# Decoder layer: one 512-wide sum moved behind a split, two norms and the mixer's adds put in another order

## The chip, the cores and the metric

The kernel runs on one core of a Trainium2 chip. The metric is device microseconds of one execution. TensorE (PE) multiplies, VectorE (DVE) and ScalarE (ACT) prepare operands and finish results, GpSimd (POOL) and SyncE (SP) mostly start transfers.

## The reference

One decoder layer on 256 tokens of width 2048: a half-step SwiGLU feed-forward (FFN, 5632 wide), a mixer with two attention branches that are gated and projected, a second half-step FFN. After each of the three parts the residual sum goes through a layer norm.

```python
def _layer_norm(x, g, b):
    mu = jnp.mean(xf, axis=-1, keepdims=True)
    var = jnp.mean(jnp.square(xf - mu), axis=-1, keepdims=True)
    return (xf - mu) * lax.rsqrt(var + LN_EPS) * g + b
...
def _swiglu(x, w_gate, w_up, w_down):
    return (jax.nn.silu(x @ w_gate) * (x @ w_up)) @ w_down
...
    y = jax.nn.sigmoid(gate_mla) * (o_mla @ w_br_mla) + jax.nn.sigmoid(gate_diff) * (o_diff @ w_br_diff)
    return y @ w_out
```

All of it is float32.

## The kernel before, in words

**Products.** Each float32 product is made of three matmuls on rounded halves (`triple`, lines 205 to 207): high by high, high by low, low by high. A matmul takes a 128x128 block of activations and 128x512 of weights. Activations are kept as 128x128 blocks with the features on the partitions, for two blocks of 128 tokens, "block 0" and "block 1".

**Splits.** Every weight block, 128x1024 (two steps of the contraction), is loaded by SP into a `raw` tile and split into two `wring` tiles: ACT casts the high part (line 152), DVE subtracts it from the raw block for the low part (line 153). The pairs come from a ring of 6 or 10. `unit` puts a block's load, its split (`prep`) and its matmuls (`now`) into a pipeline; `later(n, f)` calls f after n more such steps, and `catch_up` does the matmuls of block 1 that lag behind those of block 0.

**Order.** A scheduler of the framework orders each engine's instructions from the program and from its own costs. `tc.issue_after(i)` adds a rule: what is in its scope comes behind instruction i on that engine. It is an order, not a wait on another engine. What is issued waits for its operands, and all that stands behind it on the same engine waits too.

**Gate/up groups.** After the first two column blocks, done by `project`, the gate and up weights are taken in groups p = 1 to 10 by `Hybrid.group`, which saves products by a seven-form scheme: some products are made of sums of weight blocks (line 405, tiles `sraw`, 128x1024, steps s = 0 and 1) and of sums of activations. Groups with p % 3 != 1 are "wide": they have a third step s = 2 with a 128x512 block (tiles `eraw`, the "e" sum, split and product). Forms 5, 6 and 4 have such sums; in the FFN this makes six wide groups each, p = 2, 3, 5, 6, 8, 9. Splits there stand in a fixed line (`split_in_line`), and `behind_split(n)` puts a sum behind the n-th last split of that line. The mixer's gates and its dq, dk and dv projections use the same group with `small`, without the e part.

**Norms.** `LayerNorm.evac` adds a finished bank of the last projection to the residual rows `z` (line 749 or 751) and counts statistics. After the last one `apply` computes the root on ACT (line 661), its inverse on DVE (lines 667 to 676, `f`), scales `z` (line 784), and `rows_to_quad` turns it for the next projections: PE transposes (line 647) and ACT applies gain and shift (line 652). The rows that the next residual needs are finished with gain and shift in two DVE operations each (lines 790 and 791). A dummy root (line 743) loads ACT's table ahead of time. The first norm stands between the first FFN and the mixer, the second behind the projection `w_out`, whose products of block 1 lag those of block 0; the second FFN's gate/up products on block 0 begin meanwhile.

Of the kernel before, what the change touches and what calls it, by code (L numbers as in the profile page):

```python
# [18 lines left out]
P = 128  # L19
# [40 lines left out]
def layer_kernel(ctx: ExitStack, tc: tile.TileContext, a: dict, out: bass.AP):  # L60
# [55 lines left out]
    class Acts:  # L116
        def __init__(self, k, name, kept=()):
            self.name = name
            self.kept = kept
            self.tiles = {}  # L120
            self.ready = set()
            self.made = {}
            self.raws = {}

# [12 lines left out]
        def put(self, q, b, src, i0=0, n=4):  # L137
            hi, lo = self.quad(q, b)
            hi, lo = hi[:, i0:i0 + n, :], lo[:, i0:i0 + n, :]
            if len(src.shape) == 4:  # L140
                hi, lo = (v.rearrange("p k (i c) -> p k i c", i=4) for v in (hi, lo))
            self.made[q, b] = split(hi, lo, src)
            self.ready.update((4 * q + i0 + i, b) for i in range(n))

# [3 lines left out]

    cast = [None]

    def split(hi, lo, src):
        cast[0] = S.copy(hi, src)  # L152
        return V.tensor_tensor(out=lo, in0=src, in1=hi.bitcast(F32), op=ALU.subtract)  # L153

# [185 lines left out]
    class Hybrid:  # L340
# [14 lines left out]

        def group(self, w0, w1, done, wide=False, seeded=False):
            banks = {}
# [35 lines left out]
            def seventh(p, s):  # L393
# [7 lines left out]
                def prep():  # L401
                    t = R[src][s]
                    if add is not None and (small or p != 7):
                        with nullcontext() if small else behind_split(s + 1):
                            V.tensor_tensor(out=t, in0=t, in1=R[add[1]][s], op=ALU.add)  # L405
# [20 lines left out]
            def plain(n, j, last=False):  # L426
# [13 lines left out]
                def now():  # L440
# [202 lines left out]

    def rows_to_quad(src, b, x, q, gain=None, shift=None):
        t = tr_bank()
        for i in range(4):
            PE.transpose(t[:, i * P:(i + 1) * P], src[:, i * P:(i + 1) * P], ident)
        if gain is not None:
            full = x.raw(q, b) if q in x.kept else tmp_tile([P, 512], "full")
            for i in range(4):  # L650
                k = 4 * q + i
                S.activation(full[:, i * P:(i + 1) * P], t[:, i * P:(i + 1) * P], AF.Identity,
                             bias=shift[:, k:k + 1], scale=gain[:, k:k + 1])
            t = full
        x.put(q, b, t.rearrange("p (i t) -> p i t", i=4))

    def rstd(v, eps, n, between=None):
# [3 lines left out]
        S.activation(sd, ve, AF.Sqrt, scale=4.0)  # L661
        w = sm(n, "w")
# [43 lines left out]
    class LayerNorm:  # L706
        def __init__(self, scale, residual, g, bt, each, x=None, cols=None, at=((0, 2, 4, 6), (8, 11, 14, 17)), root_at=1):
            self.scale = scale
            self.root_at = root_at
            self.x = x  # L710
# [8 lines left out]
            self.gb = [[None, None] for _ in range(2)]  # L719
            self.applied = {}  # L720

            def rows(h, b):
# [41 lines left out]
        def apply(self, b):  # L764
# [5 lines left out]
            if self.cols is None:  # L770
# [10 lines left out]
                return  # L781
            r = rstd(mv[:, 1:2], LN_EPS, 1)
            for c in range(4):
                self.applied[b] = V.tensor_scalar(out=zs[c], in0=zs[c], scalar1=mv[:, 0:1], scalar2=r,
                                                  op0=ALU.subtract, op1=ALU.mult)
                rows_to_quad(zs[c], b, self.x, c, *self.cols)
# [9 lines left out]
    def ffn(n, x, wgu, wdn, residual, g, bt, each, first=None, between=None, nxt=None, cols=None):  # L796
        hb = {}
# [59 lines left out]
        project(wgu[0], x, KD, 512, lambda b, bank: gu_done(0, b, bank), hook=first_hook,  # L857
                between=between, behind_x=3 if n == 2 else None)
        project(wgu[1], x, KD, 512, lambda b, bank: gu_done(1, b, bank), hook=second)
        look(3, 4)  # L860
        hy = Hybrid(x, seven, KD, extra=extra)
        for p in range(1, KF // 4):
            if p == KF // 4 - 1:
                for i, q in enumerate((3, 4, 0)):
# [5 lines left out]
                     p % 3 != 1, p > 1)  # L870
        ln = LayerNorm(0.5, residual, g, bt, each, nxt, cols, ((24, 26, 48, 50), (94, 97, 100, 103)), 35)
        if n == 1:
# [164 lines left out]
    def mixer(x):  # L1037
# [71 lines left out]
        for i, f in ((0, 0), (1, 0), (0, 2)):  # L1109
            w = (a["wgm"], a["wgd"])[i]  # L1110
            hy.group(w[f], w[f + 1], lambda n, b, bank, snap, op, i=i, f=f: keep_gate(i, f + n, b, bank, snap, op),
                     False, f == 2)

# [215 lines left out]
    h2 = Acts(KD, "h2", (0, 1, 2))  # L1329
    ln = LayerNorm(1.0, res[0], a["ln2_g"], a["ln2_b"], keep(1), h2, a["ln2_cols"])  # L1330
# [91 lines left out]
```

## Time and profile before

| | us |
|---|---|
| median of 3 runs | 1981.29 |
| lowest and highest | 1980.22, 1982.05 |
| profiled execution's own time | 1981.89 |
| its span, first to last instruction | 1979.8 |
| PE busy | 1960.8 |
| DVE busy | 1756.0 |
| ACT busy | 1261.4 |
| POOL busy | 294.3 |

The profile is of one execution. Its span leaves out 2.1 us of that execution's own time. A row of a timeline gives start, duration, engine, line, operation, and out<-in; `x2` means that two like instructions stand in one row; what stands in brackets is the idle time before it and what ended that. The granted clock of PE is 0.999 over the span.

### The profile page before, as it was taken

How to read it: one execution, taken by the hardware profiler on the slowest of the kernel's cores; microseconds unless marked ns; L12 is line 12 of the kernel's file. 1: busy time of each engine (PE TensorE's matmuls, PEld its weight loads, DVE VectorE, ACT ScalarE, POOL GpSimd, SP SyncE). 2: the span in 40 equal slices, each digit the busy share in tenths (PEclk: the TensorE clock that was granted, in tenths of full speed). 3: DMA queues.
4: the chain of work that ended last, by engine and by line, in shares of the span. 5: the costliest groups of instructions: out<-in, count | busy, mean ns of one | idle time of the engine just before them, and what ended most of it. 6: DMA issues, size and time to landing. Idle time of an engine off the chain costs nothing.

```text
span 1979.8 us, 25620 instructions
## 1 busy us (share of the span) xinstructions
PE 1960.8 (99%) x8796; PEld 1621.2 (82%) x8796; DVE 1756.0 (89%) x2135; ACT 1261.4 (64%) x1637; POOL 294.3 (15%) x515
## 2 busy tenths in 40 slices
PE   9999999999999999999999999999999999999997
PEld 7888888888888798888788888878888888888886
DVE  7999999999998889998877676699999999989886
ACT  6666666766655566666667765566676666666552
POOL 0221112112100011002223120012112121121000
PEclk9999999999999999999999999999999999999999
DMA  8978888778777666677667667579888877787763
GB/s 303 292 234 272 273 257 252 226 221 316 252 231 260 216 214 242 220 250 250 219 209 249 232 216 273 183 245 289 240 290 268 243 241 238 214 323 256 245 214 125
DMA packets 144594, 484.63 MB, mean 245 GB/s; under 512 B 20640, under 2 KB 20688, under 8 KB 144464
## 3 DMA queue, kind: packets, MB, share of 16 engines
q1 hardware_dynamic: 112752, 389.60, 57.2%
q0 software_dynamic: 31712, 93.41, 17.7%
q8 instruction: 69, 1.13, 0.2%
q14 instruction: 61, 0.50, 0.1%
HBM read 454.08 MB, written 28.84 MB: 244 GB/s over the span
## 4 chain that ended last, share of the span: by engine, by line
PE 48%; DVE 3%; issue 1%; DMA 1%; ACT 1%; POOL 0%; DVEq 0%; POOLq 0%; ACTq 0%
PE mm L206 15%; PE mm L207 15%; PE mm L205 15%; DVE wring L153 2%; DVE sraw L405 1%; DMA turn<-blocks 1%; PE tr L205 0%; PE tr L207 0%; PE tr L206 0%; POOL turn L684 0%; ACT wring L152 0%; DMA turned<-turn 0%; DVE blocks L682 0%; PE tr L1229 0%; PE tr L1231 0%
## 5 line engine op out<-in xcount | busy, mean ns | idle before, releaser
L152 ACT CAST wring<-raw 128x1024 fp32r<-128x1024 f32 (+2 forms) x475 | 490.6, 1038 | 340.7 <-PE mm L207 249.4
L153 DVE TENSOR_TENSOR wring<-raw,wring 128x1024 fp32r<-128x1024 f32 (+2 forms) x475 | 566.9, 1200 | 121.1 <-ACT wring L152 118.1
L152 ACT CAST wring<-sraw 128x1024 fp32r<-128x1024 f32 x436 | 452.0, 1051 | 191.9 <-DVE sraw L405 76.5
L153 DVE TENSOR_TENSOR wring<-sraw,wring 128x1024 fp32r<-128x1024 f32 x436 | 520.9, 1218 | 26.7 <-ACT wring L152 24.6
L207 PE MATMUL mm<-wring,h 128*128 128x512 f32 (+2 forms) x1260 | 484.7, 385 | 0.0
L206 PE MATMUL mm<-wring,h 128*128 128x512 f32 (+2 forms) x1260 | 484.3, 385 | 0.1
L205 PE MATMUL mm<-wring,h 128*128 128x512 f32 (+2 forms) x1260 | 483.8, 385 | 0.4 <-ACT h L152 0.4
L206 PE MATMUL mm<-wring,xs 128*128 128x512 f32 x776 | 303.1, 391 | 1.8 <-DVE wring L153 1.2
L205 PE MATMUL mm<-wring,xs 128*128 128x512 f32 x776 | 302.3, 390 | 0.0
L207 PE MATMUL mm<-wring,xs 128*128 128x512 f32 x776 | 302.0, 389 | 0.0
L206 PEld LDWEIGHTS mm<-wring,h 128*128 128x128 f32 x1260 | 236.7, 188 | 47.7 <-DVE wring L153 1.4
L205 PEld LDWEIGHTS mm<-wring,h 128*128 128x128 f32 x1260 | 236.7, 188 | 47.4 <-ACT h L152 0.9
L207 PEld LDWEIGHTS mm<-wring,h 128*128 128x128 f32 x1260 | 236.7, 188 | 47.2 <-DVE h L153 0.7
L405 DVE TENSOR_TENSOR sraw<-sraw,sraw 128x1024 f32<-128x1024 f32 x168 | 199.3, 1217 | 3.5 <-DMA sraw<-in_wdv_dram 2.4
L206 PEld LDWEIGHTS mm<-wring,xs 128*128 128x128 f32 x776 | 145.7, 188 | 35.7 <-DVE wring L153 5.6
L205 PEld LDWEIGHTS mm<-wring,xs 128*128 128x128 f32 x776 | 145.7, 188 | 30.3
L207 PEld LDWEIGHTS mm<-wring,xs 128*128 128x128 f32 x776 | 145.7, 188 | 29.8
L206 PE MATMUL mm<-wring,x 128*128 128x512 f32 x348 | 135.9, 390 | 0.7 <-DVE wring L153 0.7
L205 PE MATMUL mm<-wring,x 128*128 128x512 f32 x348 | 135.1, 390 | 0.7 <-ACT wring L152 0.5
L207 PE MATMUL mm<-wring,x 128*128 128x512 f32 x348 | 135.3, 389 | 0.0
L684 POOL DMA_DIRECT2D hT<-blocks x176 | 96.8, 562 | 186.4 <-DVE blocks L682 186.4
L407 POOL DMA_DIRECT2D sraw<-in_gu_dram x40 | 35.5, 887 | 511.7 <-DVE sraw L405 406.2
(301 smaller groups left out, 2210.4 us busy)
## 6 DMA issues: line engine op xcount, KB each, us to landing
raw<-in_gu_dram SPq DMA_DIRECT2D x167, 512.0 KB, 5.1
sraw<-in_gu_dram SPq DMA_DIRECT2D x160, 512.0 KB, 5.3
raw<-in_dn_dram SPq DMA_DIRECT2D x140, 512.0 KB, 4.8
sraw<-in_gu_dram POOLq DMA_DIRECT2D x40, 512.0 KB, 7.0
sraw<-in_dn_dram SPq DMA_DIRECT2D x36, 512.0 KB, 6.2
hraw<-hT POOLq DMA_DIRECT2D x68, 256.0 KB, 5.7
raw<-in_w_out_dram SPq DMA_DIRECT2D x32, 512.0 KB, 4.3
eraw<-in_gu_dram SPq DMA_DIRECT2D x48, 256.0 KB, 5.7
```

Of the source, the lines that this page charges most:

```text
L152: cast[0] = S.copy(hi, src)
L153: return V.tensor_tensor(out=lo, in0=src, in1=hi.bitcast(F32), op=ALU.subtract)
L205: PE.matmul(o, xh, wh, start=first, stop=False, skip_group_check=again)
L206: PE.matmul(o, xh, wl, start=False, stop=False, skip_group_check=again)
L207: PE.matmul(o, xl, wh, start=False, stop=last, skip_group_check=again)
L405: V.tensor_tensor(out=t, in0=t, in1=R[add[1]][s], op=ALU.add)
L407: nc.gpsimd.dma_start(R["12"][s], source("22", s), accum_op=ALU.add)
L684: nc.gpsimd.dma_start(to.rearrange("(g r) (i f) -> i r g f", g=4, i=4)[i], t[32 * i:32 * (i + 1), :].rearrange("r (g f) -> r g f", g=4))
```

## The change

Four edits. In the lists below a row is a place in an engine's order, with its line and its tiles.

**Gate/up.** An e sum (s = 2) is put behind the second last split of the line and no longer behind the third last. `behind_split(s + 1)` becomes `behind_split(min(s + 1, 2))`.

DVE in form 6 of the third group (p = 3), before; `sraw_460`, `sraw_461` and `eraw_468` are the weights of the three steps, `raw_1155` is the next plain block:

```order
139 L405 TENSOR_TENSOR sraw_460<-sraw_460,sraw_464 128x1024
140 L405 TENSOR_TENSOR sraw_461<-sraw_461,sraw_465 128x1024
141 L405 TENSOR_TENSOR eraw_468<-eraw_468,eraw_469 128x512
142 L153 TENSOR_TENSOR wring_115<-sraw_460,wring_114 128x1024
143 L153 TENSOR_TENSOR wring_105<-sraw_461,wring_104 128x1024
144 L153 TENSOR_TENSOR wring_103<-eraw_468,wring_102 128x512
145 L153 TENSOR_TENSOR wring_121<-raw_1155,wring_120 128x1024
```

And now, on the same engine:

```order
139 L416 TENSOR_TENSOR sraw_460<-sraw_460,sraw_464 128x1024
140 L416 TENSOR_TENSOR sraw_461<-sraw_461,sraw_465 128x1024
141 L155 TENSOR_TENSOR wring_115<-sraw_460,wring_114 128x1024
142 L155 TENSOR_TENSOR wring_105<-sraw_461,wring_104 128x1024
143 L416 TENSOR_TENSOR eraw_468<-eraw_468,eraw_469 128x512
144 L155 TENSOR_TENSOR wring_103<-eraw_468,wring_102 128x512
145 L155 TENSOR_TENSOR wring_121<-raw_1155,wring_120 128x1024
```

The e sum moved from ahead of two splits to right ahead of its own. ACT's casts at the same place, before:

```order
115 L152 CAST wring_104<-sraw_461 128x1024
116 L152 CAST wring_102<-eraw_468 128x512
117 L152 CAST wring_116<-sraw_463 128x1024
118 L152 CAST wring_114<-eraw_468 128x512
119 L152 CAST wring_104<-sraw_466 128x1024
```

And now (`wring_102` is the pair of form 6's e block, `wring_114` here that of form 7's):

```order
115 L154 CAST wring_104<-sraw_461 128x1024
116 L154 CAST wring_116<-sraw_463 128x1024
117 L154 CAST wring_114<-eraw_468 128x512
118 L154 CAST wring_102<-eraw_468 128x512
119 L154 CAST wring_104<-sraw_466 128x1024
```

The cast of form 6's e block moved behind two others. The same stands in groups 6 and 9 and in the second FFN.

**First norm.** Its finishing steps are no longer ordered behind the scaling of block 1, and the dummy root is called at the first FFN's column 2 of block 0, without a rule. In ACT's order it now stands before the tables of the sines and exponentials, and a table load stands directly ahead of the real root. DVE at block 0's root, before:

```order
709 L153 TENSOR_TENSOR wring_103<-raw_5483,wring_102 128x1024
710 L667 RECIPROCAL y_5257<-sd_5253 128x1
711 L670 SCALAR_TENSOR_TENSOR t_5259<-y_5257,w_5255 128x1
712 L153 TENSOR_TENSOR wring_121<-raw_5500,wring_120 128x1024
713 L676 SCALAR_TENSOR_TENSOR f_5261<-t_5259,y_5257 128x1
714 L153 TENSOR_TENSOR wring_119<-raw_5516,wring_118 128x1024
```

And now; the scaling is line 808:

```order
709 L687 RECIPROCAL y_5257<-sd_5253 128x1
710 L690 SCALAR_TENSOR_TENSOR t_5259<-y_5257,w_5255 128x1
711 L696 SCALAR_TENSOR_TENSOR f_5261<-t_5259,y_5257 128x1
712 L808 TENSOR_SCALAR z_3860<-z_3860,mv_5249,f_5261 128x512 x2
713 L808 TENSOR_SCALAR z_4257<-z_4257,mv_5249,f_5261 128x512 x2
714 L155 TENSOR_TENSOR wring_121<-raw_5500,wring_120 128x1024
715 L155 TENSOR_TENSOR wring_119<-raw_5516,wring_118 128x1024
```

The two splits moved behind the scaling.

**Mixer.** The adds that finish the dq, dk and dv groups are no longer ordered behind the last split; those of the gates still are. DVE behind the dk group, before:

```order
998 L405 TENSOR_TENSOR sraw_5941<-sraw_5941,sraw_5945 128x1024
999 L153 TENSOR_TENSOR wring_105<-raw_7479,wring_104 128x1024
1000 L153 TENSOR_TENSOR wring_103<-sraw_5942,wring_102 128x1024
1001 L153 TENSOR_TENSOR wring_115<-sraw_5941,wring_114 128x1024
1002 L405 TENSOR_TENSOR sraw_5943<-sraw_5943,sraw_5945 128x1024
```

And now:

```order
1000 L416 TENSOR_TENSOR sraw_5940<-sraw_5940,sraw_5944 128x1024
1001 L416 TENSOR_TENSOR sraw_5941<-sraw_5941,sraw_5945 128x1024
1002 L155 TENSOR_TENSOR wring_105<-raw_7479,wring_104 128x1024
1003 L155 TENSOR_TENSOR wring_5068<-sraw_5940,wring_5067 128x1024
1004 L155 TENSOR_TENSOR wring_115<-sraw_5941,wring_114 128x1024
```

The split of `sraw_5942` no longer stands ahead of that of `sraw_5941`.

**Second norm.** `catch_up(0)` does all block 1 products of `w_out` before the second FFN begins. The splits of that FFN's first weights are ordered: from its fourth block behind block 0's turned rows, root and cast, from its eighth behind block 1's scaling and root. Gain and shift of every second quad are done by DVE in two 128x512 operations (lines 665 and 666). The finishing steps are spread over more steps, each behind the latest split. PE between block 0's gate/up products and block 1's transposes, before:

```order
5652 L205 MATMUL mm_10280<-wring_114,h_1436_10252 128x512
5653 L206 MATMUL mm_10280<-wring_115,h_1436_10252 128x512
5654 L207 MATMUL mm_10280<-wring_114,h_1437_10253 128x512
5655 L647 MATMUL tr_10374<-ident,z_9692 128x128 x4
5656 L647 MATMUL tr_10388<-ident,z_9692 128x128 x4
5657 L647 MATMUL tr_10400<-ident,z_9770 128x128 x4
```

And now, with the last product of `w_out` (`mm_10163`) 37 rows ahead of the transposes, where before it stood 18 ahead (row 5636):

```order
5606 L210 MATMUL mm_10163<-wring_102,y_9598 128x512
5607 L208 MATMUL mm_10371<-wring_120,h_1429_10224 128x512
...
5643 L208 MATMUL mm_10371<-wring_5067,h_1435_10250 128x512
5644 L658 MATMUL tr_10318<-ident,z_9692 128x128 x4
5645 L658 MATMUL tr_10332<-ident,z_9692 128x128 x4
5646 L658 MATMUL tr_10342<-ident,z_9770 128x128 x4
```

The last `w_out` products moved 19 products further ahead of the transposes.

The diff:

```diff
-    def project(w, x, k_tiles, width, done, k0=0, hook=None, between=None, behind_x=None):
+    def project(w, x, k_tiles, width, done, k0=0, hook=None, between=None, norm=None, free=(3, 7)):
...
-                with tc.issue_after(x.made[0, 0].ins) if behind_x is not None and j >= behind_x else nullcontext():
+                waits = ()
+                if norm is not None and j >= free[0]:
+                    if j >= free[1]:
+                        waits = norm.applied[1], norm.root[1]
+                    else:
+                        waits = norm.x.made[0, 0], norm.root[0] if j == free[0] else norm.x.cast[0, 0]
+                with ExitStack() as stack:
+                    for i in waits:
+                        stack.enter_context(tc.issue_after(i.ins))
...
-                        with nullcontext() if small else behind_split(s + 1):
+                        with nullcontext() if small else behind_split(min(s + 1, 2)):
...
-                        with behind_split(1) if small else nullcontext():
+                        with behind_split(1) if gates else nullcontext():
...
+            if shared and q % 2 == 1:
+                v, o = (u.rearrange("p (i t) -> p i t", i=4) for u in (full, t))
+                g, b0 = (u[:, 4 * q:4 * q + 4].unsqueeze(2).to_broadcast([P, 4, P]) for u in (gain, shift))
+                with tc.issue_after(x.made[q - 3, b].ins) if q > 2 else nullcontext():
+                    V.tensor_tensor(out=v, in0=o, in1=g, op=ALU.mult)
+                V.tensor_tensor(out=v, in0=v, in1=b0, op=ALU.add)
...
-            if c == 1 and b == 1:
-                later(self.root_at, root_table)
+            if self.ahead is None:
+                if (c, b) == (2, 0):
+                    S.activation(sm(1, "sq"), zero[:, 0:1], AF.Sqrt)
+            elif (c, b) == (1, 1):
+                later(self.ahead, root_table)
...
-                with tc.issue_after(self.applied[1].ins):
+                with ExitStack() as stack:
+                    for i in (self.applied[1], lows[0]) if self.ahead is not None else ():
+                        stack.enter_context(tc.issue_after(i.ins))
...
-                later(12 + c, lambda c=c: finish(c))
+                later((12 if self.ahead is None else 10 + 4 * b) + c, lambda c=c: finish(c))
...
-        project(wgu[1], x, KD, 512, lambda b, bank: gu_done(1, b, bank), hook=second)
+        project(wgu[1], x, KD, 512, lambda b, bank: gu_done(1, b, bank), hook=second, norm=norm, free=(0, 0))
...
+    catch_up(0)
 
     ffn(2, h2, a["gu2"], a["dn2"], res[1], a["ln3_g"], a["ln3_b"],
-        lambda b, c, z: nc.sync.dma_start(out[b * P:(b + 1) * P, c * 512:(c + 1) * 512], z))
+        lambda b, c, z: nc.sync.dma_start(out[b * P:(b + 1) * P, c * 512:(c + 1) * 512], z), norm=ln)
```

More of the change, by code (lines that the diff above doesn't have):

```diff
@@ L122, in __init__ @@
             self.made = {}
+            self.cast = {}
             self.raws = {}
@@ L142, in put @@
             self.made[q, b] = split(hi, lo, src)
+            self.cast[q, b] = cast[0]
             self.ready.update((4 * q + i0 + i, b) for i in range(n))
@@ L642, in run, with rows_to_quad @@
                     plain(*u, i >= len(units) - tail)
-    def rows_to_quad(src, b, x, q, gain=None, shift=None):
+    def rows_to_quad(src, b, x, q, gain=None, shift=None, shared=False):
         t = tr_bank()
@@ L649, in rows_to_quad, with rstd @@
             full = x.raw(q, b) if q in x.kept else tmp_tile([P, 512], "full")
[L650 to L653, printed above, removed]
+            if shared and q % 2 == 1:
[4 more added lines that the diff above has]
+                V.tensor_tensor(out=v, in0=v, in1=b0, op=ALU.add)
+            else:
+                for i in range(4):
+                    k = 4 * q + i
+                    S.activation(full[:, i * P:(i + 1) * P], t[:, i * P:(i + 1) * P], AF.Identity,
+                                 bias=shift[:, k:k + 1], scale=gain[:, k:k + 1])
             t = full
         x.put(q, b, t.rearrange("p (i t) -> p i t", i=4))
-    def rstd(v, eps, n, between=None):
+    def rstd(v, eps, n, between=None, root=None):
         ve = sm(n, "ve")
@@ L660, in rstd @@
         sd = sm(n, "sd")
-        S.activation(sd, ve, AF.Sqrt, scale=4.0)
+        sqrt = S.activation(sd, ve, AF.Sqrt, scale=4.0)
+        if root is not None:
+            root.append(sqrt)
         w = sm(n, "w")
@@ L706, in layer_kernel, with __init__ @@
     class LayerNorm:
-        def __init__(self, scale, residual, g, bt, each, x=None, cols=None, at=((0, 2, 4, 6), (8, 11, 14, 17)), root_at=1):
+        def __init__(self, scale, residual, g, bt, each, x=None, cols=None, at=((0, 2, 4, 6), (8, 11, 14, 17)), ahead=None):
             self.scale = scale
-            self.root_at = root_at
+            self.ahead = ahead
             self.x = x
@@ L720, in __init__ @@
             self.applied = {}
+            self.root = []
             def rows(h, b):
@@ L793, in apply, with ffn @@
             for c in range(4):
-                later(12 + c, lambda c=c: finish(c))
-    def ffn(n, x, wgu, wdn, residual, g, bt, each, first=None, between=None, nxt=None, cols=None):
+                later((12 if self.ahead is None else 10 + 4 * b) + c, lambda c=c: finish(c))
+    def ffn(n, x, wgu, wdn, residual, g, bt, each, first=None, between=None, nxt=None, cols=None, norm=None):
         hb = {}
```

19 lines of the change are left out of this document (10 added, 9 removed).

## The prediction

> **What bounds the kernel now.** I read the page's busy table first, then the busy time by stage, then each engine's order of time around the places where TensorE (PE) waits.
>
> ```profile
> span 1979.8 us, 25620 instructions
> PE 1960.8 (99%) x8796; PEld 1621.2 (82%) x8796; DVE 1756.0 (89%) x2135; ACT 1261.4 (64%) x1637; POOL 294.3 (15%) x515
> ```
>
> PE is busy in all but 19.0 us (1979.8 − 1960.8), and DVE is next with 89%. The change takes no matmul away, so it can only move those 19 us or add to them. The stages say where they lie. Columns: stretch, its length, then busy time of PE, PEld, DVE, ACT, POOL with counts, the granted clock, the DMA share, GB/s.
>
> ```profile
> 0.00:12.00 12.00, 9.53 (x41) 7.52 (x42) 4.93 (x7) 6.45 (x8) 1.54 (x9) 1.00 0.84 297
> 12.00:688.00 676.00, 675.63 (x2976) 557.92 (x2975) 630.49 (x726) 437.94 (x532) 97.59 (x163) 1.00 0.80 258
> 688.00:703.00 15.00, 13.56 (x73) 10.45 (x72) 11.96 (x26) 10.79 (x29) 0.55 (x1) 1.00 0.14 36
> ...
> 948.00:964.00 16.00, 14.26 (x63) 11.15 (x62) 16.00 (x17) 10.23 (x12) 9.06 (x17) 1.00 0.64 185
> ...
> 1274.00:1330.00 56.00, 54.66 (x253) 44.14 (x253) 51.45 (x81) 37.83 (x67) 3.88 (x8) 1.00 0.56 195
> 1330.00:1960.00 630.00, 629.53 (x2773) 519.80 (x2772) 580.71 (x633) 400.49 (x486) 94.18 (x157) 1.00 0.78 251
> 1960.00:1980.00 20.00, 9.07 (x41) 7.17 (x39) 14.84 (x32) 0.41 (x2) 0.00 (x0) 0.86 0.29 106
> ```
>
> Start and end hold 2.47 and 10.93 us, which the change leaves alone. The first norm (688 to 703) holds 1.44 us of PE's idle time, the mixer place (948 to 964) 1.74, the second norm (1274 to 1330) 1.34. Both feed-forward halves together hold 0.84. So four edits contend for under 5 us of possible gain, and a loss has no such bound.
>
> **1. Gate/up: the e sum one place later.** An e sum is the 128x512 addition of line 405; behind it come a cast on ACT (line 152) and a subtraction on DVE (line 153) before PE may use the block. First DVE, then ACT, then PE at one of six such places (third, sixth and ninth group of each feed-forward half, form 6); the last row is the sixth place.
>
> ```profile
> 141.80 2.35 DVE L405 TENSOR_TENSOR sraw<-sraw,sraw 128x1024 f32<-128x1024 f32 x2
> 144.06 0.69 DVE L405 TENSOR_TENSOR eraw<-eraw,eraw 128x512 f32<-128x512 f32 x1
> 144.66 2.35 DVE L153 TENSOR_TENSOR wring<-sraw,wring 128x1024 fp32r<-128x1024 f32 x2
> 146.94 0.68 DVE L153 TENSOR_TENSOR wring<-eraw,wring 128x512 fp32r<-128x512 f32 x1
> 147.54 1.22 DVE L153 TENSOR_TENSOR wring<-raw,wring 128x1024 fp32r<-128x1024 f32 x1
> 148.67 2.35 DVE L153 TENSOR_TENSOR wring<-sraw,wring 128x1024 fp32r<-128x1024 f32 x2
> ```
> ```profile
> 142.46 2.96 ACT L152 CAST wring<-sraw 128x1024 fp32r<-128x1024 f32 x3 [1.26 <-PE mm L207]
> ...
> 146.79 0.61 ACT L152 CAST wring<-eraw 128x512 fp32r<-128x512 f32 x1
> ```
> ```profile
> 145.20 0.61 PE L205 MATMUL mm<-wring,x 128*128 128x512 f32 x2
> 145.94 0.50 PE L206 MATMUL mm<-wring,xs 128*128 128x512 f32 x1
> ...
> 148.79 0.39 PE L206 MATMUL mm<-wring,xe 128*128 128x512 f32 x1
> ...
> 149.24 0.39 PE L206 MATMUL mm<-wring,x 128*128 128x512 f32 x1
> 151.74 0.39 PE L206 MATMUL mm<-wring,xs 128*128 128x512 f32 x1
> ...
> 1669.53 0.50 PE L206 MATMUL mm<-wring,xs 128*128 128x512 f32 x1
> ```
>
> PE starts a product every 0.23 us (two steps from 148.79 to 149.24). At 145.20 two stand at that pitch, the next would start at 145.66 and starts at 145.94, when the split that began at 144.66 has ended (1.22 alone, by the row at 147.54, so 145.88): 0.28 us are lost. The edit puts the e sum behind two splits, directly ahead of its own split, and on ACT the e cast drops behind two other casts. Worked on: the two sums end at 144.15. The first split now waits for its cast, the second of the three from 142.46, which ends at 144.46; it runs to 145.73, 0.15 earlier than 145.88. The second split ends at 146.87, the e sum runs 146.79 to 147.47. Only then can ACT cast it (0.61): 147.56 to 148.17, with 0.09 for the handover. The e split follows, 148.21 to 148.90, and the split of the raw block behind it, 148.81 to 150.02. PE wants these at 148.64 and, after two more products, at 149.1 to 149.4. Its product of 149.24 now starts at 150.08: +0.84 us, with up to 0.1 for another restart (the first product after a wait shows 0.50 instead of 0.39). Six places: +5.0 to +5.6; I take **+5.2**. Ends: −2.3 (six times 0.28 plus 0.1, if the cast slips in early) and +7.8 (six times the whole lateness of 1.3 us, 150.02 against 148.76).
>
> Behind the waiting splits DVE has those of form 7 (148.67), about 1.3 us later too. The first ends at 149.89 today and PE's first product with it is that of 151.74, 1.85 later, so these cost nothing while PE's other products from 149.24 on stand between. In the other wide groups the same e sum moves too:
>
> ```profile
> 104.17 0.68 DVE L153 TENSOR_TENSOR wring<-eraw,wring 128x512 fp32r<-128x512 f32 x1
> 107.72 0.39 PE L206 MATMUL mm<-wring,xe 128*128 128x512 f32 x1
> ```
>
> There the split ends at 104.85 and PE uses it at 107.72: 2.9 us of cover for 1.3, so nothing. The cover is PE's products on older blocks; without it these six would cost like the others. Forms 5 and 4 have their e sum behind one split more with PE far behind: nothing.
>
> **2. First norm without fixed order.**
>
> ```profile
> 685.53 0.16 DVE L667 RECIPROCAL y<-sd 128x1 f32<-128x1 f32 x1
> 687.30 0.15 DVE L676 SCALAR_TENSOR_TENSOR f<-t,y 128x1 f32<-128x1 f32 x1
> 688.50 1.91 DVE L784 TENSOR_SCALAR z<-z,mv,f 128x512 f32<-128x512 f32 x4
> ```
> ```profile
> 684.35 0.20 ACT L661 ACTIVATE sd<-ve 128x1 f32<-128x1 f32 x1
> ...
> 1304.05 1.28 ACT L807 ACT_TABLE_LOAD   x1
> 1305.35 0.39 ACT L807 ACTIVATE sg<-mm 128x256 f32<-128x256 f32 x1
> ```
> ```profile
> 689.19 1.50 PE L647 MATMUL tr<-ident,z 128*128 128x128 f32 x12 [0.48 <-DVE z L784]
> 691.41 0.66 PE L647 MATMUL tr<-ident,z 128*128 128x128 f32 x4 [0.73 <-ACT h1raw L652]
> ```
>
> Two things happen. The dummy root that loads the table early is now so early that another table follows it, so a table load of 1.28 us (the row at 1304.05 is its price) stands ahead of the real root: the reciprocal moves from 685.53 to about 685.9. But the two weight splits that stood between the reciprocal and the scaling of z now stand behind it, 2.4 us of DVE: scaling begins at about 686.6 instead of 688.50, and seven of PE's last down products now fill the time behind the transposes. The waits of 0.48 and 0.73 go (1.21). Against that, finishing steps (lines 790/791) enter block 1's chain and its scaling comes about 1 us later, which costs some 0.1: I take **−1.1**. Ends: −2.0 (the 1.44 of the stretch and restarts) and +1.3 (the whole load on the path).
>
> The Trainium skill's page "ScalarE: Activation LUTs" (What ACT_TABLE_LOAD costs) prices a switch at about 1.28 us for the load and another 1.38 us of draining. The load agrees with the 1.28 above, but the next activation follows 0.02 us behind it (1305.35), so no drain shows here; by the page this term would be about +0.3 and the sum 1.4 higher.
>
> **3. Mixer: finishing adds free of the splits.**
>
> ```profile
> 960.60 2.35 DVE L153 TENSOR_TENSOR wring<-sraw,wring 128x1024 fp32r<-128x1024 f32 x2
> 963.00 0.50 PE L206 MATMUL mm<-wring,xs 128*128 128x512 f32 x1 [0.70 <-DVE wring L153]
> ```
>
> PE waits 0.70 us for the second of these two splits. In the new order the first of the two stands behind it, so it is ready one split (1.2) earlier: the wait and its restart go, **−0.75**. Ends 0 (another block is late in its place) and −1.0. The other wait of that stretch, 1.0 us for a transposed block that ACT copies out, keeps its order: nothing.
>
> **4. Second norm.**
>
> ```profile
> 1291.65 0.69 DVE L749 TENSOR_TENSOR z<-mm,z 128x512 f32<-128x512 f32 x1 [0.29 <-PE mm L207]
> 1295.47 1.91 DVE L784 TENSOR_SCALAR z<-z,mv,f 128x512 f32<-128x512 f32 x4
> ```
> ```profile
> 1296.08 1.57 PE L647 MATMUL tr<-ident,z 128*128 128x128 f32 x12 [0.38 <-DVE z L784]
> 1298.33 0.66 PE L647 MATMUL tr<-ident,z 128*128 128x128 f32 x4 [0.69 <-ACT h2raw L652]
> 1299.19 0.50 PE L205 MATMUL mm<-wring,h 128*128 128x512 f32 x1 [0.20 <-ACT h L152]
> ```
>
> From block 1's last column (1291.65) to its transposes (1296.08) run 4.4 us. PE has 18 gate/up products of block 0 for that now (4.1 us at 0.23) and 37 in the new order (8.4 us), because all of w_out stands ahead of them. The wait of 0.38 goes. Half of the gain/shift work goes from ACT (16 small activations) to DVE (eight 128x512 operations with an operand like line 749's, 0.69 alone and 0.60 in a row: about 4.8 us more), which feeds the transposes' banks sooner and removes most of 0.69 and 0.20. With restarts I take **−1.6**. Ends: −2.0, and +3 where DVE cannot carry it: DVE has 51.45 of 56 us there, and with 4.8 more 56.25, above the stretch itself. The weight splits behind then come only 0 to 0.2 us ahead of PE by my working from the durations above, so this term is the least sure. The residual rows written behind the finishing steps leave a little later; DMA is 56% busy there: nothing.
>
> **The sum.** +5.2 − 1.1 − 0.75 − 1.6 = +1.75 us. The profiled execution took 1981.89 us (2.1 around its span), so it would take 1983.6; the three runs have their median at 1981.29, 0.6 below, and I put the forecast there: **1983.0 us**.
>
> **Rivals.** (a) The e sum's delay is hidden: ACT's cast comes with a shorter wait, or PE has a product to spare. For it speaks that six other places have 2.9 us of cover; against it that at 145.94 PE already waits on DVE, and that the chain sum, cast, split takes 0.69 + 0.61 + 0.68, 1.98 us, and nothing on DVE fills its middle. The term is then 0, sum −3.45: 1977.8 us; with the six old waits closed, 1975.6. It decides if the e split ends before PE's 148.64. (b) DVE becomes the bound of the second norm's stretch: +3 instead of −1.6, sum +6.35: 1987.6 us; for it 51.45 of 56 us, against it that the finishing steps may be put off. (c) Each of the six places costs the whole 1.3 us: sum +4.35, 1985.6 us. (d) The change of tables holds ACT for twice the load's 1.28 us, so that the first norm's term is −1.1 + 1.28 = +0.2: sum +3.05, 1984.3 us; the row at 1305.35 speaks against it. The page named above would have it nearly so.
>
> **Chances.** The forecast's case 0.45 (its own range 1981 to 1985), (a) 0.17, (b) 0.16, (c) 0.14, (d) 0.08. About 0.2%, 4 us, is what a measurement of this kernel can tell from no change, so faster means below 1977.3 and slower above 1985.3. Faster: over half of (a) and a tail of the first, 0.12. Slower: nearly all of (b), over half of (c), tails of the others, 0.31. Same: 0.57. The range from 1977 to 1988 leaves out less than half of (a) and the upper end of (b).
>
> **What would show it.** In the new profile each of the six places should have an idle of about 0.3 and one of about 0.6 us ahead of a product that waits for DVE's line 155, an e sum that starts about 2.6 us after its two large sums have ended, and DVE idle about 0.7 us for ACT's cast. Around 688 the z scaling should start about 2 us earlier against PE's last down products, behind a table load; at 962 the wait of 0.70 should be gone; from 1274 to 1330 PE should idle under 0.5 us. I am wrong in size if the e splits end ahead of PE, and wrong in sign if PE shows repeated waits for splits between 1296 and 1330 together with a DVE that never idles.

## The result, and the profile after

The changed kernel takes 1989.98 us (median of 6 runs, 1988.12 to 1990.66), the kernel before 1981.67 in the same comparison. The ratio is 1.0041 with a 95% interval of 1.0028 to 1.0054: 8.3 us slower, where 1.75 were forecast, and 2 us above the upper end of the range.

The busy table of the changed kernel, and PE's waits of the kernel before and of the changed one (engine, line, what was waited for, us in total, times, longest):

```profile
span 1986.3 us, 25576 instructions
PE 1966.7 (99%) x8796; PEld 1621.1 (82%) x8796; DVE 1763.3 (89%) x2143; ACT 1259.3 (63%) x1622; POOL 294.4 (15%) x515
```
```profile
PE mm L206 <- DVE wring L153: 1.9, 5, 0.7
...
PE tr L1156 <- ACT dkT L704: 1.0, 1, 1.0
```
```profile
PE mm L209 <- DVE wring L155: 4.0, 9, 0.8
PE mm L208 <- ACT wring L154: 2.1, 1, 2.1
...
PE tr L658 <- DVE z L808: 0.2, 1, 0.2
```

The waits at the transposes are down to 0.2 us, that at `dkT` is gone, those for splits have doubled, and one wait of 2.1 us for an ACT cast is new. PE's busy time rose by 5.9 us with the same number of matmuls, so some of them also ran longer. By stage, the changed kernel:

```profile
688.00:703.00 15.00, 14.87 (x75) 11.50 (x74) 14.61 (x33) 10.38 (x26) 2.17 (x4) 1.00 0.47 154
...
948.00:964.00 16.00, 16.00 (x73) 13.24 (x72) 16.00 (x17) 11.17 (x13) 9.85 (x19) 1.00 0.68 186
...
1274.00:1330.00 56.00, 55.85 (x260) 45.32 (x259) 53.39 (x87) 32.77 (x52) 3.81 (x7) 1.00 0.54 181
```

PE's idle time fell from 1.44 to 0.13 us at the first norm, from 1.74 to 0 in the mixer's stretch and from 1.34 to 0.15 at the second norm. All three edits closed the waits they were expected to close; that the mixer's stretch lost both of its waits is taken up with mixer_alone. What these stages leave out is the stretch behind, from 1330 to 1355; first the kernel before, then the changed one:

```profile
1330.00:1355.00 25.00, 25.00 (x112) 20.71 (x111) 23.47 (x24) 17.16 (x21) 6.62 (x11) 1.00 1.03 347
```
```profile
1330.00:1355.00 25.00, 22.11 (x87) 16.68 (x86) 20.32 (x21) 14.30 (x17) 6.71 (x11) 0.93 0.93 302
```

In the same 25 us PE starts 87 matmuls and no longer 112: 25 fewer at 0.23 us are 5.7 us. DVE is idle for 4.7 us there. The new wait in PE's timeline of the changed kernel, then in ACT's:

```profile
1342.23 0.50 PE L208 MATMUL mm<-wring,xs 128*128 128x512 f32 x1 [2.07 <-ACT wring L154]
1343.49 0.50 PE L209 MATMUL mm<-wring,xs 128*128 128x512 f32 x1 [0.76 <-DVE wring L155]
...
1344.10 0.63 PE L208 MATMUL mm<-wring,xs 128*128 128x512 f32 x1
1344.52 0.63 PE L209 MATMUL mm<-wring,xs 128*128 128x512 f32 x1
```
```profile
1339.70 1.05 ACT L154 CAST wring<-sraw 128x1024 fp32r<-128x1024 f32 x1 [3.46 <-DMA sraw<-in_gu_dram]
...
1341.13 1.05 ACT L154 CAST wring<-sraw 128x1024 fp32r<-128x1024 f32 x1
1343.53 1.99 ACT L154 CAST wring<-sraw 128x1024 fp32r<-128x1024 f32 x2 [1.35 <-DMA sraw<-in_gu_dram]
```

This is the first gate/up group of the second FFN (p = 1). ACT sits 3.46 us in front of a cast whose block is still on its way. ACT's order in the program says what stands behind. Before, and then after; `sraw_10687` and `sraw_10688` before, `sraw_10685` and `sraw_10686` after, are the two blocks that DVE has just summed for one form; `sraw_10689` and `sraw_10690` before, `sraw_10687` and `sraw_10688` after, are form 7's blocks, which come by transfer:

```
1062 CAST wring_120<-sraw_10687
1063 CAST wring_10092<-raw_10740
1064 CAST wring_118<-sraw_10688
1065 CAST wring_10090<-sraw_10689
1066 COPY snap
1067 CAST wring_104<-sraw_10690
```
```
1053 CAST wring_10092<-raw_10738
1054 CAST wring_10090<-sraw_10687
1055 COPY snap
1056 CAST wring_120<-sraw_10685
1057 CAST wring_104<-sraw_10688
1058 CAST wring_118<-sraw_10686
```

One of form 7's casts now stands ahead of each cast of a sum, and PE needs the sums first. DVE has both sums ready at 1339.06 (begun at 1336.71, 2.35 long), but ACT takes the first at 1341.13 and the second in the row of 1343.53, behind form 7's second block. In the kernel before, ACT casts each sum as soon as DVE has made it, and the transfer is waited for later, with PE still supplied:

```profile
1337.35 1.06 ACT L152 CAST wring<-sraw 128x1024 fp32r<-128x1024 f32 x1 [1.86 <-DVE sraw L405]
...
1339.26 2.00 ACT L152 CAST wring<-sraw 128x1024 fp32r<-128x1024 f32 x2
...
1342.80 1.05 ACT L152 CAST wring<-sraw 128x1024 fp32r<-128x1024 f32 x1 [1.07 <-DMA sraw<-in_gu_dram]
```

Now one of the six e places, after: DVE, ACT and PE.

```profile
141.47 2.35 DVE L416 TENSOR_TENSOR sraw<-sraw,sraw 128x1024 f32<-128x1024 f32 x2
144.16 2.36 DVE L155 TENSOR_TENSOR wring<-sraw,wring 128x1024 fp32r<-128x1024 f32 x2 [0.35 <-ACT wring L154]
146.44 0.68 DVE L416 TENSOR_TENSOR eraw<-eraw,eraw 128x512 f32<-128x512 f32 x1
147.81 0.69 DVE L155 TENSOR_TENSOR wring<-eraw,wring 128x512 fp32r<-128x512 f32 x1 [0.69 <-ACT wring L154]
148.42 1.22 DVE L155 TENSOR_TENSOR wring<-raw,wring 128x1024 fp32r<-128x1024 f32 x1
```
```profile
147.16 0.62 ACT L154 CAST wring<-eraw 128x512 fp32r<-128x512 f32 x1 [0.33 <-DVE eraw L416]
```
```profile
144.88 0.61 PE L208 MATMUL mm<-wring,x 128*128 128x512 f32 x2
...
148.56 0.50 PE L209 MATMUL mm<-wring,xe 128*128 128x512 f32 x1
...
149.70 0.50 PE L209 MATMUL mm<-wring,x 128*128 128x512 f32 x1 [0.41 <-DVE wring L155]
150.03 0.40 PE L210 MATMUL mm<-wring,x 128*128 128x512 f32 x1
```

The last of these products in the kernel before:

```profile
149.47 0.39 PE L207 MATMUL mm<-wring,x 128*128 128x512 f32 x1
```

All of it is 0.33 us earlier than before by the sums (141.47 against 141.80). With that shift the prediction's steps stand to 0.1 us: e sum at 146.46 (146.44 here), cast at 147.23 (147.16), e split at 147.88 (147.81), raw split ended at 149.69 (149.64). From the pair of products at 144.88 to that at 149.70 are 4.82 us, before 4.04 (145.20 to 149.24): +0.78. The product behind it loses another 0.1 us, since it comes 0.33 us after the one that waited and not 0.23. So the place costs 0.89 (0.56 from 149.47 to 150.03, and the shift of 0.33), where 0.84 and up to 0.1 for a restart were worked out.

And the first norm after, ACT and DVE:

```profile
686.93 1.28 ACT L679 ACT_TABLE_LOAD   x1
688.23 0.20 ACT L679 ACTIVATE sd<-ve 128x1 f32<-128x1 f32 x1
```
```profile
688.46 0.17 DVE L687 RECIPROCAL y<-sd 128x1 f32<-128x1 f32 x1 [0.29 <-ACT sd L679]
...
689.11 1.92 DVE L808 TENSOR_SCALAR z<-z,mv,f 128x512 f32<-128x512 f32 x4
```

The load stands ahead of the root, the reciprocal waits 0.29 us for it, and the scaling follows 0.65 us behind the reciprocal instead of 2.97 (685.53 to 688.50 before). The root starts 0.02 us after the load's end: no drain of 1.38 us stands behind it, as the prediction said against that rule of the Trainium skill ("ScalarE: Activation LUTs", What ACT_TABLE_LOAD costs).

By the profiles the span grew by 6.5 us. Where it grew can be read from the start of one and the same product in both:

| the product stands | before | after | PE is later by |
|---|---|---|---|
| ahead of the first e place | 143.16 | 142.84 | −0.32 |
| behind the first FFN's three e places | 686.05 | 688.61 | 2.56 |
| behind the first norm and the gates | 939.93 | 940.77 | 0.84 |
| behind the mixer place and the attention | 1269.96 | 1268.67 | −1.29 |
| behind the second norm and the group at 1340 | 1348.98 | 1351.64 | 2.66 |
| behind the second FFN's three e places | 1950.09 | 1956.15 | 6.06 |

The first 0.32 us lie ahead of all four edits. The two FFNs lose 2.88 and 3.40 us, and six times 0.89 are 5.3 of that; the other 1.0 is not traced further. The first norm with the gates gains 1.72 and the mixer place with the attention 2.13. From the second norm to behind the group PE takes 82.97 us (1268.67 to 1351.64) where it took 79.02: 3.95 more, the 5.7 less what the norm gains. The last 0.4 us come behind these products. The profiled run is also the shortest of the six, 1.9 us below their median.

### The profile page after: what moved, and what is told of

Its sections match the earlier page's. It is cut to its first block, busy times and chain, and to the rows that moved or that the text cites. A ratio compares the mean times of both kernels' runs of the same rounds, so it can differ in the third digit from the quotient of the medians.

```text
span 1986.3 us, 25576 instructions
## 1 busy us (share of the span) xinstructions
PE 1966.7 (99%) x8796; PEld 1621.1 (82%) x8796; DVE 1763.3 (89%) x2143; ACT 1259.3 (63%) x1622; POOL 294.4 (15%) x515
## 4 chain that ended last, share of the span: by engine, by line
PE 86%; DVE 6%; issue 3%; DMA 2%; ACT 2%; POOL 0%; SPq 0%; DVEq 0%; ACTq 0%; POOLq 0%
PE mm L209 27%; PE mm L210 27%; PE mm L208 27%; DVE wring L155 3%; ACT wring L154 2%; DMA sraw<-in_gu_dram 1%; PE tr L209 1%; PE tr L208 1%; PE tr L210 1%; DVE sraw L416 1%; PE tr L658 0%; DMA raw<-in_gu_dram 0%; DMA sraw<-in_wgm_dram 0%; DVE eraw L416 0%; PE tr L1255 0%
```

## The experiments

Theory 1: the six e places cost what was worked out, and the rest of the loss is ACT's order at the second FFN's first group, which DVE's 4.8 us more of gain and shift bring about through the scheduler. Theory 2: the wait at 1340 comes from transfers that are late in any order, because the residual rows and the weight loads leave later. Medians of 11 runs (after: 6); the kernel before had 1981.6 to 1981.9 beside each.

| kernel | median us | ratio to before, 95% interval |
|---|---|---|
| after | 1989.98 | 1.0041 (1.0028 to 1.0054) |
| e_undone | 1983.58 | 1.0006 (0.9998 to 1.0015) |
| norm2_undone | 1984.46 | 1.0012 (1.0003 to 1.0020) |
| cast_line | 1981.50 | 0.9995 (0.9986 to 1.0004) |
| shared_undone | 1983.28 | 1.0006 (0.9997 to 1.0015) |
| norm2_alone | 1985.45 | 1.0020 (1.0011 to 1.0028) |
| mixer_alone | 1979.89 | 0.9993 (0.9984 to 1.0001) |
| norm1_alone | 1979.84 | 0.9990 (0.9982 to 0.9999) |
| norm1_late_table | 1980.81 | 0.9998 (0.9989 to 1.0007) |
| best_shared | 1977.28 | 0.9980 (0.9971 to 0.9989) |
| best_plain | 1976.94 | 0.9976 (0.9968 to 0.9985) |
| best_cast | 1981.48 | 0.9998 (0.9989 to 1.0007) |
| best_both | 1980.85 | 0.9996 (0.9987 to 1.0005) |

**The e sum back in its place** (e_undone)

```diff
-                        with nullcontext() if small else behind_split(min(s + 1, 2)):
+                        with nullcontext() if small else behind_split(s + 1):
```

> The changed kernel with the e sum back behind the split it stood behind before; all else as changed. Theory 1 (six e places cost 0.9 us each, and a new wait of about 5.5 us in the second FFN's first group comes from ACT's order there): the six waits behind the e splits go and the old 0.28 us waits come back, so 5.2 to 5.7 us less than the changed kernel, about 2.5 to 3 us above the kernel before. Theory 2 (the new wait comes from transfers that arrive late, whatever ACT's order): the same here, since the e sum has no part in either. If the e places cost nothing to the end of the kernel (given back later), no change.

Measured: 6.4 us less than the changed kernel, 2.0 above the kernel before. The e edit costs 6.4 us by these medians, a little more than the 5.2 to 5.7 expected; the medians come from different comparisons, so the excess is not read further. The cost is not given back later.

**The second-norm edit undone** (norm2_undone) and **alone** (norm2_alone)

```diff
-                waits = ()
-                if norm is not None and j >= free[0]:
...
+                waits = (norm.x.made[0, 0],) if norm is not None and free[0] == 3 and j >= 3 else ()
...
-                rows_to_quad(zs[c], b, self.x, c, *self.cols, self.ahead is not None)
+                rows_to_quad(zs[c], b, self.x, c, *self.cols)
...
-                    for i in (self.applied[1], lows[0]) if self.ahead is not None else ():
+                    for i in (self.applied[1],) if self.ahead is not None else ():
...
-                later((12 if self.ahead is None else 10 + 4 * b) + c, lambda c=c: finish(c))
+                later(12 + c, lambda c=c: finish(c))
...
-    catch_up(0)
```

The second kernel has this edit alone and the e sum, the mixer and the first norm as before.

> The changed kernel with the whole second-norm edit undone (catch-up, ordered splits, DVE's half of gain and shift, spread finishing steps). Both theories: the wait at the second FFN's first group goes (5.5 us by the new profile) and the old waits of the second norm come back (1.1 us), so 4 to 6 us less than the changed kernel, 2 to 4 us above the kernel before.

> The kernel before with the second-norm edit alone. Theory 1: the new wait at the second FFN's first group stands without the other edits, 5.5 to 6.7 us, less 1.1 us of closed waits in the second norm: 4.4 to 5.6 us above the kernel before. If the wait needs the other edits too (their shift in time), 1 us below the kernel before.

Measured: undone, 5.5 us less than the changed kernel; alone, 3.6 us more than the kernel before, somewhat under the 4.4 expected. In the latter's trace the wait stands as in the changed kernel; first the stage, then PE:

```profile
1330.00:1355.00 25.00, 21.85 (x83) 17.10 (x82) 19.84 (x21) 13.71 (x16) 6.73 (x11) 0.86 0.92 293
```
```profile
1343.05 0.80 PE L208 MATMUL mm<-wring,xs 128*128 128x512 f32 x1 [2.69 <-ACT wring L154]
```

So the edit alone makes it. At the norm itself it gains (0.16 us of idle instead of 1.34), 10 us later it loses more: from the second norm to behind the group, between the same two products as in the table above, PE takes 83.90 us here (1268.87 to 1352.77) and 79.02 in the kernel before.

**ACT's casts in the order of the splits** (cast_line)

```diff
-            line.append(split(*a))
+            with tc.issue_after(line_cast[-1].ins) if strict and line_cast else nullcontext():
+                line.append(split(*a))
+            line_cast.append(cast[0])
```

> The changed kernel with one rule more: in the gate/up groups ACT's casts of the weight blocks stand in the order of the splits, so that form 7's casts no longer stand ahead of those of the sums of form 5 or 6. Theory 1 (ACT waits for form 7's transfer while the finished sums stand behind it): the wait of 2.1 and 0.8 us and the slower products behind it go, 4 to 5.5 us less than the changed kernel; the six e places keep their cost. Theory 2 (transfers late in any order): within 1 us of the changed kernel.

Measured: 8.5 us less than the changed kernel, at the time of the kernel before. Theory 2 falls: all four edits are kept, and a rule on the order of ACT's casts mends the time. From the second norm to behind the group PE takes 78.94 us (1269.05 to 1347.99), no more than before. The transfers are no earlier: POOL starts the first of form 7's loads at 1332.16 (1331.14 in the changed kernel), and the cast of the second begins at 1344.55, when its block is there (1343.53 in the changed kernel). ACT still waits for a transfer, but behind the sums' casts, and PE's wait shrinks to 0.62 us:

```profile
1339.04 2.18 ACT L154 CAST wring<-sraw 128x1024 fp32r<-128x1024 f32 x2 [0.57 <-DVE sraw L419]
...
1344.55 1.05 ACT L154 CAST wring<-sraw 128x1024 fp32r<-128x1024 f32 x1 [1.42 <-DMA sraw<-in_gu_dram]
```
```profile
1341.40 0.50 PE L209 MATMUL mm<-wring,xs 128*128 128x512 f32 x1 [0.62 <-DVE wring L155]
```

The gain is larger than the 4 to 5.5 us expected. The rule also reorders the casts at the e places, so the time of this kernel does not measure the wait alone. The profiles differ by 5.1 us (1986.3 to 1981.2) and the medians by 8.5: the profiled run of the changed kernel is the shortest of its six, 1.9 us below their median, and that of this one the longest of its eleven, 1.4 above.

**Gain and shift back on ACT** (shared_undone)

```diff
-                rows_to_quad(zs[c], b, self.x, c, *self.cols, self.ahead is not None)
+                rows_to_quad(zs[c], b, self.x, c, *self.cols)
```

> The changed kernel with gain and shift of all quads back on ACT, the finishing steps still spread and the residual rows still written late. In its order ACT casts the two sums ahead of form 7's blocks again. Theory 1: 3 to 5 us less than the changed kernel (the wait goes, up to 1 us comes back at the second norm's transposes). Theory 2: the wait stays, since the late residual rows and loads stay: within 1 us of the changed kernel.

Measured: 6.7 us less than the changed kernel. In its program ACT casts the sums ahead of form 7's blocks again, and the stage is full, though the finishing steps are spread as in the changed kernel:

```profile
1330.00:1355.00 25.00, 25.00 (x112) 20.70 (x111) 24.20 (x25) 17.40 (x21) 5.81 (x10) 1.00 1.00 331
```

The second norm keeps its gain without DVE's share (0.23 us idle). From the second norm to behind the group PE takes 77.88 us (1268.99 to 1346.87), 1.1 less than before. So the eight DVE operations bought nothing there, and with them gone the order and the wait are gone. Against the expectation form 7's loads are earlier here too (the first starts at 1328.57), so this run alone would not tell the two theories apart; cast_line, where they are later, does. That the operations act through the scheduler's own reckoning of DVE's time is argued, not shown.

**The mixer edit alone** (mixer_alone)

```diff
-                        with behind_split(1) if small else nullcontext():
+                        with behind_split(1) if gates else nullcontext():
```

> The kernel before with the mixer edit alone. By the prediction 0.75 us less; by the new profile, in which both waits at 950 and 962 are gone, 1.9 us less, or about 1 us less where the wait at 791 grows as in three of the four runs so far.

Measured: 2.0 us less than the kernel before, with an interval that just reaches no change. Both waits of that stretch are gone, also the one at `dkT` that the prediction had stay. Its order is the same; its time is not. First the kernel before, then this one; the first row of each is an earlier cast, the second the copy:

```profile
941.05 1.05 ACT L152 CAST wring<-sraw 128x1024 fp32r<-128x1024 f32 x1 [3.05 <-DMA sraw<-in_wdv_dram]
...
951.34 0.61 ACT L704 COPY dkT<-turned 128x512 f32<-128x512 f32 x1
```
```profile
939.09 1.05 ACT L154 CAST wring<-sraw 128x1024 fp32r<-128x1024 f32 x1 [1.61 <-DMA sraw<-in_wdv_dram]
...
949.38 0.62 ACT L719 COPY dkT<-turned 128x512 f32<-128x512 f32 x1
```

The copy comes 1.96 us earlier, and so does the cast for whose block ACT waits ahead of it. PE's transposes start at 950.29 without a wait (952.00 before). But this is not shown to be the edit's doing. norm2_alone has the order of the kernel before on every engine up to the second norm, and PE there waits at the second place only:

```profile
950.94 0.44 PE L1179 MATMUL tr<-dkT,dqT 128*128 128x128 f32 x2
...
961.88 0.50 PE L209 MATMUL mm<-wring,xs 128*128 128x512 f32 x1 [0.70 <-DVE wring L155]
```

So the wait of 0.70 us goes with the edit, while that at `dkT` comes and goes with the landing of a block, in the same order.

**The first-norm edit alone** (norm1_alone), and **without the early table** (norm1_late_table)

```diff
-            if self.ahead is None:
-                if (c, b) == (2, 0):
-                    S.activation(sm(1, "sq"), zero[:, 0:1], AF.Sqrt)
-            elif (c, b) == (1, 1):
-                later(self.ahead, root_table)
+            if (c, b) == (1, 1):
+                later(35 if self.ahead is None else self.ahead, root_table)
```

The diff shows the second of the two against the first.

> The kernel before with the first-norm edit alone. By the prediction 1.1 us less; if the table load falls on the path, up to 0.3 us more than the kernel before. The new profile shows 1.0 us of waits closed around 688.

> The kernel before with the first-norm edit without its early dummy root: the dummy keeps its old place and rule, only the finishing steps are free. In its order the two weight splits stand again between the reciprocal and the scaling, and no table load stands ahead of the root. If the gain of the first-norm edit comes from the splits that moved (the prediction's step), it is gone: within 0.7 us of the kernel before. If the freed finishing steps give it, 1 us or more below the kernel before, since 1.28 us of table load are saved beside.

Measured: 2.0 us less than the kernel before with the early table, 1.0 less without, which its interval does not tell from no change. From 688 to 703 PE is busy for 14.98 us with the table and 13.57 without. In the latter's trace the splits stand between reciprocal and scaling again, and PE waits as before:

```profile
685.05 0.15 DVE L682 RECIPROCAL y<-sd 128x1 f32<-128x1 f32 x1
...
688.04 1.91 DVE L800 TENSOR_SCALAR z<-z,mv,f 128x512 f32<-128x512 f32 x4
```
```profile
688.73 1.50 PE L653 MATMUL tr<-ident,z 128*128 128x128 f32 x12 [0.50 <-DVE z L800]
```

So the early dummy, which costs a table load of 1.28 us in front of the root, is what moves the splits and closes the waits; freeing the finishing steps alone leaves them.

**What is left when the two losses go** (best_shared, best_plain). best_shared is the changed kernel with the e sum back and gain and shift on ACT; best_plain also has the finishing steps in their old places.

```diff
-                    for i in (self.applied[1], lows[0]) if self.ahead is not None else ():
+                    for i in (self.applied[1],) if self.ahead is not None else ():
...
-                later((12 if self.ahead is None else 10 + 4 * b) + c, lambda c=c: finish(c))
+                later(12 + c, lambda c=c: finish(c))
```

The diff is that of best_plain against best_shared.

> The changed kernel with two parts undone: the e sum back in its place, and gain and shift back on ACT (so that ACT casts the sums ahead of form 7's blocks). Theory 1: what is left are the gains, 1.0 (first norm), 1 to 1.9 (mixer) and 1.1 (second norm): 3 to 4 us below the kernel before. If the gains are given back later: no change.

> As best_shared, and the finishing steps of the second norm not spread (their old rule and places): of the second-norm edit only the catch-up and the order of the splits are left. If these two give the second norm's gain, as best_shared: 3.5 to 4.6 us below the kernel before. If the spread gives it, 2.5 to 3.5 below.

Measured: 4.6 and 4.9 us less than the kernel before, and both beat it with their whole interval. Between the two there is no difference to be told, so of the second-norm edit the catch-up and the order of the splits carry the gain; the spread gives nothing.

**The cast rule instead** (best_cast: changed kernel, e sum back, casts in the order of the splits; best_both: best_shared with that rule).

> The changed kernel with the e sum back in its place and ACT's casts in the order of the splits; DVE's half of gain and shift stays. Theory 1: the wait at the second FFN's first group shrinks from over 5 to about 1.4 us as in cast_line, so 2 to 3.5 us below the kernel before. If DVE's 4.8 us more are a bound of their own, not below it.

> best_shared with ACT's casts in the order of the splits. Theory 1: nothing is left for the rule to mend there, so within 1 us of best_shared.

Measured: 0.4 and 1.0 us less than the kernel before, and so both expectations missed: best_both is 3.6 us slower than best_shared. The rule has a price at the six e places. PE there in best_cast, and in best_shared:

```profile
144.57 0.39 PE L208 MATMUL mm<-wring,xs 128*128 128x512 f32 x1
145.56 0.50 PE L209 MATMUL mm<-wring,xs 128*128 128x512 f32 x1 [0.60 <-DVE wring L155]
```
```profile
144.41 0.61 PE L208 MATMUL mm<-wring,x 128*128 128x512 f32 x2
145.15 0.50 PE L209 MATMUL mm<-wring,xs 128*128 128x512 f32 x1
```

In best_cast PE has no product ready between 144.57 and 145.56, since the raw block's cast, whose high products filled that time, stands behind the sums' casts. That is some 0.5 us at each of six places, 3 us. A rule that mends one place on ACT hurts six others.

## Why the prediction was wrong

**The e sum** was right in mechanism and size. The steps came within 0.1 us at the place shown, six times 0.89 are 5.3 us where 5.2 was the term, and putting the sum back took 6.4 us off. Rival (a), that it would be hidden, is out.

**The first norm** was right: −1.1 forecast, 1.3 us of idle gone, and the run alone is 2.0 faster, though there 0.8 us of the wait at `dkT` went as well (0.23 us is left). The table load did what was said: the reciprocal waits 0.29 us for the root, and no drain follows. Rival (d) is out.

**The mixer** was right in what it named: the wait of 0.70 us goes, −0.75 was forecast. The run alone is 2.0 us faster, but its interval, from 3.2 less to 0.2 more, holds 0.75 too. That the wait at `dkT` also went does not refute "keeps its order: nothing", since it went in norm2_alone without the edit. That the profile of the kernel before had this wait and the changed one had not is chance, as far as the runs show.

**The second norm** failed, and with it the sum. The term was −1.6 with an upper end of +3; alone it is +3.6. Inside its stretch the idle time went from 1.34 to 0.15 us, as worked out, with no wait for a split. DVE was busy for 53.39 us there (51.45 before), less than the 56.25 that the prediction had as the danger. The step that failed is that the term was closed at 1330 us, with nothing put down for the group behind. The 4.8 us of DVE work were priced as work for DVE, as rival (b) did too, and not as a change of order elsewhere. ACT's order at the next group had changed, and was not among the places read: each of two casts of blocks still in transfer stood in front of a cast of a finished sum. That place costs 5.7 us by the count of products. Rival (b) came near its size (1987.6 us) but not by its mechanism: DVE did not become the bound, it was idle for 3.14 us of that wait:

```profile
1342.20 1.23 DVE L155 TENSOR_TENSOR wring<-sraw,wring 128x1024 fp32r<-128x1024 f32 x1 [3.14 <-ACT wring L154]
```

**The range** ended at 1988 and the chance of slower was 0.31. Its bounds came from the stretches that the edits name; none allowed for a reordering outside them. The sum with the term that was missed, 1.75 + 5.7, is 7.5 us, near the 8.3 measured.

## What to carry to other kernels

When a scheduler sets the order, the price of an edit isn't closed at the end of its own stage: compare the order of every engine up to where it is the same again, and look on in-order engines for an instruction that waits on a transfer and now stands in front of ready work. Where work is moved to another engine to relieve one, ask whether the wait is still there without the move; here the catch-up and the order of the splits closed it, and the move only cost. Two losses hid three gains of 1 to 2 us each, so it paid to run the parts alone. And a wait in one profile need not belong to the order: that at `dkT` was gone in another kernel with the same order up to there.

## What the hardware showed that was not expected

After the waits of 2.07 and 0.76 us, with a single product between them, PE's products came 0.42 to 0.43 us apart instead of 0.23 (1344.10 to 1344.52). The granted clock of the changed kernel, the last but two of the columns, shows why:

```profile
1343.00:1346.00 3.00, 2.51 (x6) 1.57 (x7) 1.50 (x3) 2.47 (x3) 1.65 (x3) 0.66 0.91 352
1346.00:1350.00 4.00, 3.94 (x14) 2.71 (x14) 4.00 (x5) 2.88 (x4) 2.73 (x6) 0.82 0.53 121
```

A clock of 0.66 over 3 us and of 0.82 over 4 makes some 3.5 us at half clock, in which 1.7 us of products are lost. In e_undone, with waits of 2.72 and 0.68 us at the same place, the clock is 0.72 from 1340 to 1343, 0.50 to 1346 and 0.73 to 1350, some 6.8 us at half. So stalls of 2.8 us in all cost about twice themselves here (5.7 us by the count of products, 5.1 by the stretch of shared_undone, 82.97 against 77.88). A wait of 1.74 us in another place (best_plain, in the mixer) left the clock at 1.00:

```profile
788.00:795.00 7.00, 5.26 (x24) 4.01 (x23) 7.00 (x7) 4.58 (x5) 0.09 (x1) 1.00 0.58 187
```

The Trainium skill's page "TensorE: Matmul & The Clock Gate" (Part 1: The HAM clock gate) has the half clock follow an idle window of about 3.4 us. The halving agrees; in the changed kernel it came after 2.8 us of waiting that was broken by a product, so here a shorter and interrupted idle time was enough.
